# Longer buffers in the ring of split weights, and attention outputs placed elsewhere in memory

## The chip, the cores and the metric

The kernel runs on one core of a Trainium2 chip. The metric is the time of one execution in device microseconds (us), as the median of several runs. Besides the timed runs there is one profiled execution, whose trace the rows below come from; its own time stands beside its span in the table.

## What is computed

Two transformer-like blocks follow one another on 256 tokens of width 1024 (plus 16 learned tokens ahead of them), all in fp32. Cut to what matters here:

```python
# first block
proj = rms_norm(h) @ w_in                       # two convolution branches follow
h = h + concat(norm(y_sc), norm(y_cf)) @ w_out
hn = rms_norm(h)
idx, gates = route(hn @ w_q, sub_keys)          # top 16 of 16384 experts for each of 8 heads
act = gelu(einsum(u[idx], hn))
h = h + einsum(act * gates, v[idx])             # u and v: 16384 x 1024
# second block
proj = rmsnorm(h) @ w_in_2                      # 6144 columns: two attentions
y_sb, y_df = o_sb @ w_br_sb, o_df @ w_br_df     # outputs of the two attentions
merged = gates_a * y_sb + gates_b * y_df
h = h + merged @ w_out_2
h = h + (silu(hn @ w_ffn_gate) * (hn @ w_ffn_up)) @ w_ffn_down
```

The kernel multiplies with all 16384 experts and lets the gates be zero elsewhere, so that `u` and `v` are two matrices of 128 pieces each.

## The kernel before

Every weight matrix is cut into units of 128 x 1024 fp32 numbers; there are 454 of them, in an order written out in the list `units`. A unit goes through three rings of buffers. SyncE's queue loads it into one of 5 buffers `raw`. ScalarE copies it, rounded, into one of 3 buffers `hi` (line 152), and VectorE writes what the rounding left into one of 3 buffers `lo` (line 154). A product is then three matmuls: hi with hi, hi with lo, lo with hi, added in PSUM. Activations are kept in such pairs too: `hT` (input of `q`, `u`, `fg` and `fu`), `xT` and `xT2` (inputs of the two first projections, with 272 columns to a chunk), `osb` and `odf` (the outputs of the two attentions, inputs of `ysb` and `ydf`).

Two helpers issue nearly all matmuls. In `mm_w` the unit is the stationary operand, 128 columns at a time, and the activations stream past it:

```python
for k in range(KC):                                   # 8 chunks of 128
    ks = slice(k * P, (k + 1) * P)
    nc.tensor.matmul(ps, hi[:, ks], ahi[:, k, cols], ...)   # L183
    nc.tensor.matmul(ps, hi[:, ks], alo[:, k, cols], ...)   # L184
    nc.tensor.matmul(ps, lo[:, ks], ahi[:, k, cols], ...)   # L185
```

In `mm_a` (L197 to L199) the unit streams, 512 columns at a time, past 128 columns of activations: `v` past `w_hi` and `w_lo`, `fd` past `f_hi` and `f_lo`, `o` past `mghi` and `mglo`, `wo` past `yhi` and `ylo`. While one matmul streams, TensorE loads the stationary operand of the next, so that two reads of the core's working memory run side by side.

TensorE and SyncE follow the order in which the code is written; the other engines' order comes from a scheduler. Between the matmuls of `u` some small ones stand: the scores `sc`, and from about 370 us on the gates `gp` (L712), in the middle of every unit.

Where a tile lies is decided by pools, which place tiles one behind another. In bytes from the start of a partition, before the change: `hThi` 11168 and `hTlo` 8192 bytes behind it; the three `hi` buffers 48608, 52704, 56800; the three `lo` buffers 60896, 64992, 69088; `w_hi` 204256 (two buffers of 2048 bytes); `osbhi` 121696; `odfhi` 138080; `xT2hi` 103200; the first `f_hi` 110368; `mghi` 170848; `yhi` 182048. The buffers of a ring are 4096 bytes apart.

Of the kernel before, what the change touches and what calls it, by code (L numbers as in the profile page):

```python
# [9 lines left out]
F32 = mybir.dt.float32  # L10
F32R = mybir.dt.float32r
# [8 lines left out]
P = 128  # L20
D = 1024
# [14 lines left out]
XN = 2  # L36
WARM = 9
SOON = 60

_VECS = [  # L40
    ("norm_mix_g", 8), ("norm_mix_g_2", 8), ("b_gate_2", 16),
# [11 lines left out]
def two_blocks(ctx, tc, x, feats, vecs, w_in, w_out, w_q, keys, u, v, final_g, meta2, w_in2, lams, w_gate,  # L53
# [3 lines left out]
    const = ctx.enter_context(tc.tile_pool(name="const", bufs=1))  # L57
    wraw = ctx.enter_context(tc.tile_pool(name="wraw", bufs=5))
    whi = ctx.enter_context(tc.tile_pool(name="whi", bufs=3))
    wlo = ctx.enter_context(tc.tile_pool(name="wlo", bufs=3))  # L60
# [4 lines left out]
    def phase(name):  # L65
        st = ExitStack()
        pool = st.enter_context(tc.tile_pool(name=name, bufs=1, reuse_waits="tile"))
        return st, pool

    def mm_tile(name):  # L70
        return pmm.tile([P, 512], F32, tag="mm", name=name)
# [42 lines left out]
    loaded, ready, used = [], [], [0]  # L114
    held, latest = [], {}

    def queued(after):
        st = ExitStack()
        for i in after:
            st.enter_context(tc.issue_after(i.ins))  # L120
        return st

    def soon(i):
        return tc.high_priority(offset=SOON) if 30 <= i < 172 else ExitStack()

# [12 lines left out]

    def split_part(half):
        if half == 0:  # L140
            ready.append((whi.tile([P, D], F32R, tag="hi", name="hi0"), wlo.tile([P, D], F32R, tag="lo", name="lo0")))
        hs = slice(half * 512, (half + 1) * 512)
        hi, lo = (o[:, hs] for o in ready[0])
        nc.scalar.activation(hi, loaded[0][:, hs], AF.Copy)
        nc.vector.tensor_tensor(lo, loaded[0][:, hs], hi.bitcast(F32), op=ALU.subtract)

    def split_to(n):
        while len(ready) < min(n, len(units)):
            i = len(ready)
            with queued(held), soon(i):  # L150
                hi = whi.tile([P, D], F32R, tag="hi", name=f"hi{i}")
                latest["hi"] = nc.scalar.activation(hi, loaded[i], AF.Copy)  # L152
                lo = wlo.tile([P, D], F32R, tag="lo", name=f"lo{i}")
                latest["lo"] = nc.vector.tensor_tensor(lo, loaded[i], hi.bitcast(F32), op=ALU.subtract)  # L154
            ready.append((hi, lo))

    def unit(ahead=2):
        n = used[0]
        used[0] += 1
        load_to(n + 5)  # L160
        split_to(n + 1 + ahead)
        held.clear()
        return ready[n]
# [131 lines left out]


    s_x, px = phase("px")
    s_c, pc = phase("pc")
    load_part(0)
    load_part(1)  # L300
# [22 lines left out]
    for c in range(KC):  # L323
        g = col("norm_mix_g", c)
        nc.scalar.activation(xT[0][:, c, :], xf[:, c, :], AF.Copy, scale=g)
        nc.vector.scalar_tensor_tensor(xT[1][:, c, :], xf[:, c, :], g, xT[0][:, c, :].bitcast(F32),
                                       op0=ALU.mult, op1=ALU.subtract)
        if c in (1, 3):
            split_part(c // 2)
    split_to(2)  # L330
    for c in range(0, KC, 2):
        nc.scalar.activation(sq[:, c:c + 2, :], xf[:, c:c + 2, :], AF.Square)
# [183 lines left out]


    s_a, pa = phase("pa")
    NA = 96
    ew = [pa.tile([P, T // 4, NA, 4], F32, tag="ewa", name="ewa"), None]  # L520
# [5 lines left out]

    lm = pr.tile([P, 4, 64], F32, tag="lm", name="lm")
    nc.sync.dma_start(lm, lams.broadcast_to((P, 4, 64)))
    lam = const.tile([P, 1], F32, tag="lam", name="lam")
    sg8 = const.tile([P, 1], F32, tag="sg8", name="sg8")  # L530

    vals_a = pr.tile([P, 2, NH, TOPK], F32, tag="vals", name="vals")
    pos_a = pr.tile([P, 2, NH, TOPK], U32, tag="pos", name="pos")
# [312 lines left out]
    s_q, pq = phase("pq")  # L846
# [43 lines left out]
    NQ = sum(QN)  # L890
    QS = slice(NM, L)

    osb = (pq.tile([P, NH, T], F32R, tag="osbhi", name="osbhi"), pq.tile([P, NH, T], F32R, tag="osblo", name="osblo"))
    odf = (pq.tile([P, NH, T], F32R, tag="odfhi", name="odfhi"), pq.tile([P, NH, T], F32R, tag="odflo", name="odflo"))
    gate = pq.tile([P, 16, T], F32, tag="gate", name="gate")
    s_sb, psb = phase("psb")
# [362 lines left out]
```

## Time and profile before

| | |
|---|---|
| median of 3 runs | 1456.65 us (1452.66 to 1460.02) |
| the profiled execution | 1458.39 us |
| its span, first to last instruction | 1456.4 us |
| mean granted TensorE clock | 0.997 of full speed |
| TensorE busy (matmul) | 1437.3 us, 99% of the span |
| VectorE, ScalarE busy | 72%, 51% |
| matmuls in the trace | 10114 |

The span is 2.0 us short of the execution's own time, and that execution lies 1.7 us above the median. A matmul's duration in the trace runs from its start to its modelled end, and matmuls overlap: one of 256 columns is listed with some 0.28 us while the next starts about 0.115 us after it. What a matmul costs is therefore the distance between two starts, not its listed duration.

### The profile page before, as it was taken

To read this page: it belongs to the slowest core of one execution; us is meant where nothing else is said; L and a number is where in the kernel's file an instruction comes from. 1 tells how busy PE (TensorE), PEld (TensorE's weight loads), DVE (VectorE), ACT (ScalarE), POOL (GpSimd) and SP (SyncE) were. 2 spreads that over 40 slices of the span, in tenths; PEclk is the share of its full clock that TensorE was granted. 3 is DMA by queue.
4 is the path that set the end of the run, shared out by engine and by line. 5 is a ranking of instruction groups with operands and counts; after the bars stand their busy time and mean duration, and the time that the engine had idled before them with its cause. 6 is when DMAs were issued, how large, how long until landed. Compare 5 with 4: busy or idle time off the path is not lost.

```text
span 1456.4 us, 25587 instructions
## 1 busy us (share of the span) xinstructions
PE 1437.3 (99%) x10114; PEld 1340.5 (92%) x10114; DVE 1050.6 (72%) x1887; ACT 742.9 (51%) x1236; POOL 14.5 (1%) x35
## 2 busy tenths in 40 slices
PE   8999999999999999999999999999999999999998
PEld 8988999999999999888888888899999999899997
DVE  8997789894988999655555565675577776765666
ACT  7555444554444444444444544564455674554444
POOL 0010000000000000000000000000000000000000
PEclk9999999999999999999999999999999999999999
DMA  7525655666444444566666676654344456556562
GB/s 242 198 73 185 183 181 176 193 196 194 147 138 137 145 136 141 174 189 200 190 189 200 190 249 196 189 174 129 119 130 131 131 174 188 165 185 195 184 197 103
DMA packets 69816, 248.96 MB, mean 171 GB/s; under 512 B 7744, under 2 KB 9152, under 8 KB 69696
## 3 DMA queue, kind: packets, MB, share of 16 engines
q1 hardware_dynamic: 68256, 242.61, 53.5%
q0 software_dynamic: 1152, 4.19, 0.8%
q8 instruction: 79, 1.29, 0.4%
q10 hardware_dynamic: 288, 0.52, 0.1%
q14 instruction: 41, 0.34, 0.1%
HBM read 245.20 MB, written 2.10 MB: 170 GB/s over the span
## 4 chain that ended last, share of the span: by engine, by line
PE 92%; DVE 6%; issue 1%; ACT 0%; DMA 0%; SPq 0%; DVEq 0%; ACTq 0%
PE v L198 8%; PE v L197 8%; PE v L199 8%; PE u L183 7%; PE u L185 7%; PE u L184 7%; PE gp L712 4%; DVE lo L154 2%; PE fg L184 1%; PE fg L185 1%; PE fg L183 1%; PE fu L184 1%; PE fu L183 1%; PE fu L185 1%; PE fd L199 1%; PE fd L198 1%
## 5 line engine op out<-in xcount | busy, mean ns | idle before, releaser
L154 DVE TENSOR_TENSOR lo<-raw,hi 128x1024 fp32r<-128x1024 f32 x453 | 551.7, 1223 | 250.1 <-ACT hi L152 248.1
L152 ACT ACTIVATE hi<-raw 128x1024 fp32r<-128x1024 f32 x453 | 476.4, 1057 | 429.8 <-PE u L184 124.8
L183 PE MATMUL u<-hThi,hi 128*128 128x256 f32 x1024 | 297.3, 290 | 0.0
L185 PE MATMUL u<-hThi,lo 128*128 128x256 f32 x1024 | 286.9, 280 | 0.1
L184 PE MATMUL u<-hTlo,hi 128*128 128x256 f32 x1024 | 286.5, 280 | 0.0
L199 PE MATMUL v<-hi,w_lo 128*128 128x512 f32 x512 | 199.2, 389 | 0.0
L198 PE MATMUL v<-lo,w_hi 128*128 128x512 f32 x512 | 199.2, 389 | 0.0
L197 PE MATMUL v<-hi,w_hi 128*128 128x512 f32 x512 | 199.2, 389 | 0.0
L185 PEld LDWEIGHTS u<-hThi,lo 128*128 128x128 f32 x1024 | 193.7, 189 | 0.6 <-DVE lo L154 0.3
L184 PEld LDWEIGHTS u<-hTlo,hi 128*128 128x128 f32 x1024 | 194.2, 190 | 0.0
L183 PEld LDWEIGHTS u<-hThi,hi 128*128 128x128 f32 x1024 | 192.8, 188 | 0.0
L197 PEld LDWEIGHTS v<-hi,w_hi 128*128 128x128 f32 x512 | 96.1, 188 | 20.0
L199 PEld LDWEIGHTS v<-hi,w_lo 128*128 128x128 f32 x512 | 96.1, 188 | 20.0
L198 PEld LDWEIGHTS v<-lo,w_hi 128*128 128x128 f32 x512 | 96.1, 188 | 19.7
L712 PE MATMUL gp<-ga,gb 128*128 128x128 f32 x512 | 74.8, 274 | 0.0
L712 PEld LDWEIGHTS gp<-ga,gb 128*128 128x128 f32 x512 | 66.2, 190 | 0.0
L810 ACT ACTIVATE w_hi<-ewa 128x512 fp32r<-128x512 f32 x48 | 30.4, 633 | 65.9 <-PE v L198 65.9
L812 DVE TENSOR_TENSOR w_lo<-ewa,w_hi 128x512 fp32r<-128x512 f32 x48 | 33.2, 692 | 38.6 <-ACT w_hi L810 38.6
L184 PE MATMUL fg<-hTlo,hi 128*128 128x256 f32 x176 | 48.9, 278 | 0.4 <-DVE hTlo L245 0.4
L183 PE MATMUL fg<-hThi,hi 128*128 128x256 f32 x176 | 48.9, 278 | 0.3 <-ACT hThi L244 0.3
L185 PE MATMUL fg<-hThi,lo 128*128 128x256 f32 x176 | 48.9, 278 | 0.0
L183 PE MATMUL fu<-hThi,hi 128*128 128x256 f32 x176 | 48.7, 277 | 0.0
(409 smaller groups left out, 2949.8 us busy)
## 6 DMA issues: line engine op xcount, KB each, us to landing
raw<-in_u_dram SPq DMA_DIRECT2D x128, 512.0 KB, 3.6
raw<-in_v_dram SPq DMA_DIRECT2D x128, 512.0 KB, 3.6
raw<-in_w_in_dram SPq DMA_DIRECT2D x67, 512.0 KB, 3.6
raw<-in_w_fg_dram SPq DMA_DIRECT2D x22, 512.0 KB, 4.2
raw<-in_w_fu_dram SPq DMA_DIRECT2D x22, 512.0 KB, 3.6
raw<-in_w_fd_dram SPq DMA_DIRECT2D x22, 512.0 KB, 4.5
raw<-in_w_out_dram SPq DMA_DIRECT2D x16, 512.0 KB, 3.6
raw<-in_w_q_dram SPq DMA_DIRECT2D x16, 512.0 KB, 4.1
```

What stands on the lines that cost most here:

```text
L152: latest["hi"] = nc.scalar.activation(hi, loaded[i], AF.Copy)
L154: latest["lo"] = nc.vector.tensor_tensor(lo, loaded[i], hi.bitcast(F32), op=ALU.subtract)
L183: nc.tensor.matmul(ps, hi[:, ks], ahi[:, k, cols], start=(k == 0), stop=False)
L184: nc.tensor.matmul(ps, hi[:, ks], alo[:, k, cols], start=False, stop=False)
L185: nc.tensor.matmul(ps, lo[:, ks], ahi[:, k, cols], start=False, stop=(k == KC - 1))
L197: nc.tensor.matmul(ps, ahi[:, ts], hi[:, bs], start=first and n == 0, stop=False)
L198: nc.tensor.matmul(ps, ahi[:, ts], lo[:, bs], start=False, stop=False)
L199: nc.tensor.matmul(ps, alo[:, ts], hi[:, bs], start=False, stop=end)
L712: nc.tensor.matmul(p3[:, :, i], b[:, i, :], a[:, i, :], start=True, stop=True)
L810: nc.scalar.activation(hi, a, AF.Copy)
L812: nc.vector.tensor_tensor(lo, a, hi.bitcast(F32), op=ALU.subtract)
```

## The change

Each tile of the rings `hi` and `lo` gets 16 more fp32 numbers (64 bytes) that nothing uses, so that the buffers of a ring are 4160 bytes apart. The two small constants `lam` and `sg8` become two columns of one tile, which takes 32 bytes less. Two unused tiles, of 576 and 896 bytes, are placed ahead of `osb` and `odf`.

```diff
+SKEW = 16
+OSB, ODF = 576, 896
...
+    def fill(pool, n, name):
+        pool.tile([P, n // 4], F32, tag=name, name=name)
+
+    def ring(pool, tag, name):
+        return pool.tile([P, D + SKEW], F32R, tag=tag, name=name)[:, :D]
...
-                hi = whi.tile([P, D], F32R, tag="hi", name=f"hi{i}")
+                hi = ring(whi, "hi", f"hi{i}")
                 latest["hi"] = nc.scalar.activation(hi, loaded[i], AF.Copy)
-                lo = wlo.tile([P, D], F32R, tag="lo", name=f"lo{i}")
+                lo = ring(wlo, "lo", f"lo{i}")
...
-    lam = const.tile([P, 1], F32, tag="lam", name="lam")
-    sg8 = const.tile([P, 1], F32, tag="sg8", name="sg8")
+    lam_sg = const.tile([P, 2], F32, tag="lam_sg", name="lam_sg")
+    lam, sg8 = lam_sg[:, 0:1], lam_sg[:, 1:2]
...
+    fill(pq, OSB, "osb_at")
     osb = (pq.tile([P, NH, T], F32R, tag="osbhi", name="osbhi"), pq.tile([P, NH, T], F32R, tag="osblo", name="osblo"))
+    fill(pq, ODF, "odf_at")
     odf = (pq.tile([P, NH, T], F32R, tag="odfhi", name="odfhi"), pq.tile([P, NH, T], F32R, tag="odflo", name="odflo"))
```

After it, in bytes: `hThi` 11168 as before; `hi` 48576, 52736, 56896; `lo` 61056, 65216, 69376; `w_hi` 204608; `osbhi` 122624; `odfhi` 139904; `xT2hi` 103552; the first `f_hi` 110720; `mghi` 172672. Everything allocated behind `sg8` thus lies at a multiple of 64 bytes where it lay 32 bytes past one, except `yhi` and `ylo` of the second branch, where it is the other way round; `hT` stays 32 bytes past one.

No instruction is added, and the order of TensorE, VectorE, GpSimd and SyncE is the same. One pair moves: the two copies of the 16 learned tokens into `xT2`. On ScalarE before, where `hi267` to `hi299` are the last units of `v`, 33 splits of such units stand behind them:

```order
L152 ACTIVATE hi265_9260<-raw265_9218 128x1024
L810 ACTIVATE w_hi94_9276<-ewa_1330 128x512
L152 ACTIVATE hi266_9282<-raw266_9240 128x1024
L849 ACTIVATE xT2hi_10008<-m2hi_1022 128x8x16
L849 ACTIVATE xT2lo_10009<-m2lo_1023 128x8x16
L152 ACTIVATE hi267_9300<-raw267_9258 128x1024
```

On ScalarE after, one split of a unit of `v` (`hi299`) stands behind them:

```order
L160 ACTIVATE hi297_9899<-raw297_9857 128x1024
L818 ACTIVATE w_hi126_9915<-ewb_4410 128x512
L160 ACTIVATE hi298_9921<-raw298_9879 128x1024
L857 ACTIVATE xT2hi_10007<-m2hi_1022 128x8x16
L857 ACTIVATE xT2lo_10008<-m2lo_1023 128x8x16
L160 ACTIVATE hi299_9939<-raw299_9897 128x1024
L295 ACT_TABLE_LOAD
```

They moved 32 units later on the same engine, and nothing else changed places.

## Rows read from the trace of the kernel before

**Rows 1.** The page: busy time of each engine, and TensorE's clock in 40 slices.

```profile
span 1456.4 us, 25587 instructions
...
PE 1437.3 (99%) x10114; PEld 1340.5 (92%) x10114; DVE 1050.6 (72%) x1887; ACT 742.9 (51%) x1236; POOL 14.5 (1%) x35
...
PEclk9999999999999999999999999999999999999999
```

**Rows 2.** The page: shares of the chain that ended last.

```profile
PE 92%; DVE 6%; issue 1%; ACT 0%; DMA 0%; SPq 0%; DVEq 0%; ACTq 0%
```

**Rows 3.** TensorE, timeline of a unit of `q`: start, duration (us).

```profile
190.43 0.28 PE L185 MATMUL q<-hThi,lo 128*128 128x256 f32 x1
...
193.26 0.28 PE L185 MATMUL q<-hThi,lo 128*128 128x256 f32 x1
```

**Rows 4.** The same, for a unit of `u` some 95 us later.

```profile
285.42 0.28 PE L185 MATMUL u<-hThi,lo 128*128 128x256 f32 x1
...
288.14 0.28 PE L185 MATMUL u<-hThi,lo 128*128 128x256 f32 x1
```

**Rows 5.** TensorE's groups, 124 to 247 us: count, busy us, mean ns of one, idle.

```profile
L184 PE MATMUL u<-hTlo,hi 128*128 128x256 f32 x230 | 64.6, 281 | 0.0
...
L184 PE MATMUL q<-hTlo,hi 128*128 128x256 f32 x96 | 27.9, 291 | 0.0
```

**Rows 6.** The same, 250 to 302 us.

```profile
L184 PE MATMUL u<-hTlo,hi 128*128 128x256 f32 x113 | 31.2, 276 | 0.0
```

**Rows 7.** The same, 370 to 585 us.

```profile
L184 PE MATMUL u<-hTlo,hi 128*128 128x256 f32 x453 | 127.3, 281 | 0.0
L185 PE MATMUL u<-hThi,lo 128*128 128x256 f32 x453 | 127.1, 281 | 0.0
L712 PE MATMUL gp<-ga,gb 128*128 128x128 f32 x496 | 72.4, 274 | 0.0
```

**Rows 8.** TensorE's groups over the whole span, by shape: matmuls of 256 and 272 columns.

```profile
L185 PE MATMUL u<-hThi,lo 128*128 128x256 f32 x1024 | 286.9, 280 | 0.1
L184 PE MATMUL u<-hTlo,hi 128*128 128x256 f32 x1024 | 286.5, 280 | 0.0
...
L184 PE MATMUL fg<-hTlo,hi 128*128 128x256 f32 x176 | 48.9, 278 | 0.4 <-DVE hTlo L245 0.4
...
L185 PE MATMUL fu<-hThi,lo 128*128 128x256 f32 x176 | 48.6, 276 | 0.0
...
L184 PE MATMUL g<-xT2lo,hi 128*128 128x256 f32 x128 | 35.9, 281 | 0.0
...
L399 PE MATMUL conv<-up,diag 128*128 128x256 f32 x86 | 18.9, 378 | 0.0
...
L184 PE MATMUL ydf<-odflo,hi 128*128 128x256 f32 x64 | 18.0, 282 | 0.0
L185 PE MATMUL ysb<-osbhi,lo 128*128 128x256 f32 x64 | 18.0, 281 | 0.0
...
L184 PE MATMUL ps_sk<-xT2lo,hi 128*128 128x272 f32 x64 | 18.5, 288 | 0.0
```

**Rows 9.** The same view: matmuls of 512 columns, where the unit streams.

```profile
L199 PE MATMUL v<-hi,w_lo 128*128 128x512 f32 x512 | 199.2, 389 | 0.0
L198 PE MATMUL v<-lo,w_hi 128*128 128x512 f32 x512 | 199.2, 389 | 0.0
L197 PE MATMUL v<-hi,w_hi 128*128 128x512 f32 x512 | 199.2, 389 | 0.0
...
L198 PE MATMUL fd<-lo,f_hi 128*128 128x512 f32 x88 | 34.7, 394 | 0.0
...
L199 PE MATMUL wo<-hi,ylo 128*128 128x512 f32 x32 | 12.7, 398 | 0.8 <-DVE ylo L469 0.8
...
L199 PE MATMUL o<-hi,mglo 128*128 128x512 f32 x32 | 12.6, 394 | 0.0
```

**Rows 10.** TensorE, timeline in the middle of `v`.

```profile
601.31 0.39 PE L199 MATMUL v<-hi,w_lo 128*128 128x512 f32 x1
...
606.07 0.39 PE L199 MATMUL v<-hi,w_lo 128*128 128x512 f32 x1
```

**Rows 11.** TensorE, timeline of six fp32 passes of the convolution, merged.

```profile
34.72 1.46 PE L399 MATMUL conv<-up,diag 128*128 128x256 f32 x6
```

**Rows 12.** ScalarE, timeline around the two copies; in brackets the idle time ahead.

```profile
848.48 0.29 ACT L849 ACTIVATE xT2hi<-m2hi 128x128 fp32r<-128x128 f32 x1
848.67 0.29 ACT L849 ACTIVATE xT2lo<-m2lo 128x128 fp32r<-128x128 f32 x1
849.93 1.06 ACT L152 ACTIVATE hi<-raw 128x1024 fp32r<-128x1024 f32 x1 [0.96 <-PE v L199]
```

More of the change, by code (lines that the diff above doesn't have):

```diff
@@ L140, in split_part @@
         if half == 0:
-            ready.append((whi.tile([P, D], F32R, tag="hi", name="hi0"), wlo.tile([P, D], F32R, tag="lo", name="lo0")))
+            ready.append((ring(whi, "hi", "hi0"), ring(wlo, "lo", "lo0")))
         hs = slice(half * 512, (half + 1) * 512)
```

## The prediction

> **What bounds the kernel now.** I read the page first: TensorE is busy 99% of the span, at full clock in every slice [rows 1], and the chain that ended last is 92% TensorE [rows 2]. VectorE at 72% and ScalarE at 51% have room. So the time is the number of matmuls, which stays, times the distance from one start to the next, and the change can act only on that distance.
>
> So I went to the timeline. In a unit of `q`, 24 matmuls take from 190.43 to 193.26 us [rows 3]: 2.83 us / 24 = 118 ns each. In a unit of `u`, with the same tile `hT`, the same rings and the same 256 columns, 24 take from 285.42 to 288.14 us [rows 4]: 113.3 ns. The groups say the same: a listed duration of 281 ns goes with 118 and one of 276 ns with 113.3, so a difference between listed means is a difference between distances wherever nothing is waited for. By that measure the stretch from 124 to 247 us runs at 281 throughout, that from 250 to 302 us at 276 [rows 5, 6], and that from 370 to 585 us, with gates in the middle of each unit, at 281 again [rows 7]. Other engines do not explain a pace that stays put for 120 us. What I read in it: two reads of working memory run side by side in TensorE, the streaming operand and the next stationary one; they can settle into a rhythm without collisions or into one with them; and the rhythm survives from unit to unit.
>
> **What the rhythm could have to do with addresses.** Chunks of a unit are 512 bytes apart and chunks of `hT` 1024, so unit address minus activation address, modulo 512, is the same for all chunks. Before, all six buffers share it: `hT` 64, `osb` and `odf` 128, `v` 0, `fd` 192, `o` 128, `wo` 192 (worked out from the addresses above; `xT2` has chunks 1088 bytes apart and sweeps through all multiples of 64). The rows beside it: distance 0 gives 389 ns for 512 columns in all three lines of `v`, while 128 and 192 give 394 to 398 [rows 9]; `v` takes 4.76 us for 21 matmuls, 226.7 ns each [rows 10]. Distance 128 gives 281 to 282 at 256 columns (`ysb`, `ydf`), the sweep 281 (`g`), distance 64 both 276 and 281, and in `fg` and `fu` nearly always the good one, 276 to 278 [rows 8]. After, the six differ: `hT` sees 32, 160, 96 from `hi` and 224, 352, 288 from `lo`; `v` sees 128, 256, 192 and 320, 448, 384; `osb` 192, 320, 256 and 384, 0, 448; `odf` 320, 448, 384 and 0, 128, 64 (in the order of the three buffers' use).
>
> **The change part by part.** I use 276.2 ns (48.6 us / 176) as the good duration.
>
> `u`: L184 and L185 have 286.5 and 286.9 us for 1024 each, 280.0 ns, so 3.8 ns over; for three lines, 3072 x 3.8 = 11.7 us at most. Of this, the stretch with gates holds 452 x 3 x 4.8 = 6.5 us, and the rest 5.2. `q`: 96 of its 128 in each line lie in the slow stretch, 288 x 4.8 = 1.4 us (its listed 291 contains waits). If the collisions live on because every unit lies at the same distance, distances that change from unit to unit should break them up. Bounds: 0 and 13.1 us. I take all of 5.2 and 1.4, since `fu` shows that the good rhythm can hold for long, and half of 6.5, since the gates restart the stream in every unit and it may fall either way. 9.9 us.
>
> `ysb` and `ydf`: 384 matmuls, 5.3 ns over: 2.0 us at most, 0 at least; I take 2.0, as these two tiles are both moved and skewed.
>
> `v`: 0. It runs at its best row now and can gain nothing from a better rhythm. Bound on the other side: 1536 x 5 ns (394 - 389) = 7.7 us, with `wo`'s 398 13.8 us. `fg` and `fu`: 0, bound 1056 x 4 = 4.2 us of loss. `fd`, `o`, `wo`: 456 matmuls, +-5 ns, 2.3 us either way; 0. `g` and the 272-column projections sweep before and after: 0.
>
> The two copies moved on ScalarE take 0.29 us each and stand ahead of an idle time of 0.96 us [rows 12]; later they delay the split of unit 299 by at most 0.59 us, and splits run two units of 5.4 us (24 x 226.7 ns) ahead. Nothing, unless that lead were gone: then 0.6 us. The merged constants and the unused tiles add no instruction. Writing rings at other addresses could change VectorE's and ScalarE's own durations, which the trace can't show; with both engines off the chain [rows 2] I take 0.
>
> Sum: 9.9 + 2.0 = 11.9 us. 1458.4 - 11.9 = 1446.5 for an execution like the profiled one; that one lies 1.7 above the median, so 1445.
>
> One rule speaks against all of it. The Trainium skill, "TensorE: Matmul & The Clock Gate", section "Step-by-step: what each phase is for", says that TensorE has two independent read ports and that loading the next weights takes no read bandwidth from the running matmul. By that the sum would be 0. That the same matmul on the same tiles goes at 113.3 and 118 ns [rows 3, 4] shows that something disturbs it, though not that it is the other read.
>
> **The rivals.** *Slower: `v` loses its rhythm.* `v` is the one long stream at distance 0, and every 512-column stream at another distance is slower by 5 to 9 ns [rows 9]. After the change none of the six buffers is at 0 from `w_hi`. Then `v` pays 7.7 us; if `fg` and `fu` go to 281 as well, 4.2; if `u` and `q`, instead of gaining, run wholly at 281 to 282, 3456 x 1.3 = 4.5. All three are one mechanism, that only a constant, fortunate distance keeps a rhythm free of collisions: 7.7 + 4.2 + 4.5 = 16.4, so 1473. With my gain in `u` kept, it decides from 11.9 us / 1536 = 7.7 ns on a matmul of `v`. For it: `v`, `fd`, `o` and `wo`. Against: the slow stretch of `u` at a constant distance.
>
> *No change.* Either distances don't matter, and the two paces come from how a stream started (the unchanged addresses of rows 3 and 4 speak for it), or `u` gains what `v` loses (11.9 - 7.7 = 4.2): 1452 to 1457.
>
> *Much faster: a lower floor.* Nearly all tiles but `hT` move from 32 bytes past a multiple of 64 to a multiple of 64. Were 113.3 and 226.7 ns themselves the price of that offset, `v` would fall. How far, bounded by the row that streams slowest per column: a pass of the convolution, six of which take 1.46 us with a tail of 378 ns [rows 8, 11], starts every 216 ns. `v` at 216 saves 1536 x 10.7 = 16.4 us, with the 11.9 above 1428. No row before has an aligned stream in this format, so nothing speaks for or against it directly. The same page, section "Back-to-back issue gap", has N/2.4 + 2.5 ns, or 216 ns for 512 columns and 109 for 256; by its figures `v` would save an estimated 16.9 us. Distances of exactly 113.3 and 226.7 disagree with it before the change.
>
> **How the numbers follow.** Forecast (1439 to 1449) 0.34; much faster 0.11; no change or an even trade (1449.5 to 1464) 0.26; slower 0.29. 0.5% is 7.3 us, about what can be told from no change. Faster is the forecast and the lower floor, 0.45; slower is the rival, 0.29; same 0.26. The range reaches from the lower floor's 1428 to the rival's 1474 and leaves out under 2 in 10 in the tails (a lower floor in the other streams too, or `v` at `wo`'s 398). The forecast's own range is 1439 to 1449.
>
> **What would show it.** Right: `u`'s L184 and L185 at 276 to 278 instead of 280, also from 370 to 585 us; `ysb` and `ydf` at 276 to 278; `v` at 389; clock and order as before. Wrong: `v` at 393 or more (the rival), `u` still at 280 or more, or a listed duration below 276 or 389 (the lower floor). The step I trust least is that varied distances break up a collision rhythm in `u` and leave `v` alone: `v`'s own row is the evidence against it.

## The result, and the profile after

| | before | after |
|---|---|---|
| median of 4 runs (before: the 3 above and one more) | 1457.77 us (1452.66 to 1460.02) | 1470.67 us (1469.51 to 1473.88) |
| profiled execution, its span | 1458.39, 1456.4 us | 1473.88, 1471.8 us |
| mean granted TensorE clock | 0.997 | 0.995 |

The ratio is 1.0095, with a 95% interval from 1.0069 to 1.012: slower, by 0.95%, where the forecast was faster. The median lies inside the stated range, but 21 us above the forecast's own (1439 to 1449). The page after, the engines' line and the chain:

```profile
span 1471.8 us, 25586 instructions
...
PE 1454.7 (99%) x10114; PEld 1353.7 (92%) x10114; DVE 1051.2 (71%) x1887; ACT 742.6 (50%) x1236; POOL 15.6 (1%) x35
...
PE 92%; DVE 5%; ACT 1%; DMA 1%; issue 1%; SPq 0%; POOL 0%; DVEq 0%; ACTq 0%
```

TensorE is the bound as before, with as many matmuls, and busy 17 us longer; VectorE and ScalarE have the same work in the same time. The groups of TensorE by shape (busy us, mean ns of one), which answer to [rows 8, 9]; lines have moved by 8:

```profile
L193 PE MATMUL u<-hThi,lo 128*128 128x256 f32 x1024 | 288.1, 281 | 0.0
L192 PE MATMUL u<-hTlo,hi 128*128 128x256 f32 x1024 | 287.9, 281 | 0.0
L206 PE MATMUL v<-lo,w_hi 128*128 128x512 f32 x512 | 201.5, 393 | 0.4 <-DVE lo L162 0.4
L205 PE MATMUL v<-hi,w_hi 128*128 128x512 f32 x512 | 200.8, 392 | 0.0
L207 PE MATMUL v<-hi,w_lo 128*128 128x512 f32 x512 | 200.7, 392 | 0.0
...
L192 PE MATMUL fg<-hTlo,hi 128*128 128x256 f32 x176 | 49.5, 281 | 0.4 <-DVE hTlo L253 0.4
...
L193 PE MATMUL fu<-hThi,lo 128*128 128x256 f32 x176 | 49.3, 280 | 0.0
...
L192 PE MATMUL ydf<-odflo,hi 128*128 128x256 f32 x64 | 17.9, 280 | 0.0
```

`v` has gone from 389 to 392 or 393, `fu` from 276 to 280, `fg` from 278 to 281, and `u`, forecast at 276 to 278, to 281. The pace itself is in the timeline of TensorE after, a stretch of `u` and the first two units of `v`:

```profile
283.82 0.28 PE L191 MATMUL u<-hThi,hi 128*128 128x256 f32 x1
...
292.35 0.28 PE L191 MATMUL u<-hThi,hi 128*128 128x256 f32 x1
...
600.73 0.39 PE L205 MATMUL v<-hi,w_hi 128*128 128x512 f32 x1
...
606.25 0.40 PE L205 MATMUL v<-hi,w_hi 128*128 128x512 f32 x1
```

The first two rows are three units apart, 72 matmuls: 8.53 us / 72 = 118.5 ns, where [rows 4] had 113.3 in this part of the span. The last two are 24 matmuls apart: 230.0 ns, where [rows 10] had 226.7.

Where the time went, by the first start of a stage in the two traces (us):

| stage | before | after | difference |
|---|---|---|---|
| up to `q` | 124.21 | 123.72 | -0.5 |
| `q` and `u`, up to `v` | 472.6 | 477.0 | +4.4 |
| `v`, up to `ps_sq` | 351.2 | 357.5 | +6.3 |
| projections and `g`, up to `ysb` | 247.5 | 249.2 | +1.7 |
| `ysb`, `ydf`, `o`, up to `fg` | 70.9 | 70.5 | -0.4 |
| `fg`, `fu`, `fd`, to the end | 190.0 | 193.9 | +3.8 |

The sum is 15.4 us (before rounding), the difference of the two spans. The +1.7 of the projections is not the change's. The stretches after (PEclk is the granted clock as a share of 2.4 GHz):

```profile
core 0: us, PE busy (x) PEld busy (x) DVE busy (x) ACT busy (x) POOL busy (x), PEclk, DMA share, GB/s
950.00:958.00 8.00, 7.40 (x40) 5.87 (x38) 6.79 (x12) 5.00 (x12) 0.31 (x1) 1.00 0.43 131
958.00:959.30 1.30, 0.61 (x4) 0.24 (x2) 1.30 (x3) 1.29 (x3) 0.24 (x1) 1.00 0.19 38
959.30:963.50 4.20, 4.20 (x23) 4.20 (x24) 4.05 (x5) 1.40 (x2) 0.00 (x0) 0.59 0.65 204
963.50:970.00 6.50, 6.50 (x55) 6.50 (x54) 5.09 (x15) 5.34 (x13) 0.53 (x1) 1.00 0.66 229
```

Behind a start of `ps_sq` with little work ahead (0.61 us in 1.3), the clock stood at 0.59 for 4.2 us, most of it at its lower level of 1.2 GHz: 15 matmuls 0.213 us apart instead of 0.118, with the two at its edges 1.6 us. The same place in the kernel before, with as little work ahead (0.49 us in 1.1), and in the kernels with one half of the change kept the full clock. So 13.8 us remain for the change in this profile, and 12.9 between the medians.

### The profile page after: what moved, and what is told of

The parts are those of the page before. It is cut to its first block, busy times and chain, and to the rows that moved or that the text cites. A ratio compares the mean times of both kernels' runs of the same rounds, so it can differ in the third digit from the quotient of the medians.

```text
span 1471.8 us, 25586 instructions
## 1 busy us (share of the span) xinstructions
PE 1454.7 (99%) x10114; PEld 1353.7 (92%) x10114; DVE 1051.2 (71%) x1887; ACT 742.6 (50%) x1236; POOL 15.6 (1%) x35
## 4 chain that ended last, share of the span: by engine, by line
PE 92%; DVE 5%; ACT 1%; DMA 1%; issue 1%; SPq 0%; POOL 0%; DVEq 0%; ACTq 0%
PE v L206 8%; PE v L205 8%; PE v L207 8%; PE u L191 7%; PE u L192 7%; PE u L193 7%; PE gp L720 4%; DVE lo L162 1%; PE fg L192 1%; PE fu L191 1%; PE fu L192 1%; PE fu L193 1%; PE fg L191 1%; PE fg L193 1%; PE fd L207 1%; PE fd L206 1%
## 5 line engine op out<-in xcount | busy, mean ns | idle before, releaser
L192 PE MATMUL fu<-hTlo,hi 128*128 128x256 f32 x176 | 49.5, 281 | 0.0
```

Source lines behind the costliest of these rows:

```text
L192: nc.tensor.matmul(ps, hi[:, ks], alo[:, k, cols], start=False, stop=False)
```

## The experiments

The theories: *changing* (distances that differ from buffer to buffer keep TensorE out of its free rhythm), *distance* (each distance of unit and activation has a pace of its own), *alignment* (multiples of 64 bytes). Distances are unit minus activation, modulo 512. A pace is called free when it is the fastest that was seen, 113.3 ns for 256 columns and 226.7 for 512. Each ratio is to the kernel before as timed on the same chip beside that run. Its median there was 1451.37 us for the first four experiments, 1454.5 for those from the skew of 256 bytes to the moved stages, 1454.79 for the first two versions with kicks and 1455.6 for the last two.

**The skew undone.** The changed kernel with one number altered.

```diff
-SKEW = 16
+SKEW = 0
```

> The changed kernel with ring buffers 4096 bytes apart again; the merged constants (everything behind them at a multiple of 64 bytes) and the two fills stay. Distance of unit minus activation, modulo 512, is the same for all buffers again: 32 for hT, 0 for v, 64 for osb, 192 for odf. Theory 'changing' (the loss comes from distances that differ from buffer to buffer, which keep TensorE from settling): v back at 389 ns, u at 276 to 281, fg and fu at 276 to 279, time 1452 to 1461. Theory 'alignment' (the loss comes from tiles at multiples of 64 bytes): v at 392 to 393, u, fg and fu at 281, time 1468 to 1474. Theory 'distance' (a value of its own for each distance, 0 the only free one): v at 389, but u, fg and fu at 281 since 32 is not 0; time about 1463.

1467.31 us, ratio 1.0108 (1.0077 to 1.0140).

```profile
L192 PE MATMUL u<-hTlo,hi 128*128 128x256 f32 x1024 | 287.7, 281 | 0.0
L207 PE MATMUL v<-hi,w_lo 128*128 128x512 f32 x512 | 199.2, 389 | 0.0
...
L192 PE MATMUL fu<-hTlo,hi 128*128 128x256 f32 x176 | 49.4, 281 | 0.0
```

`v`, back at the constant distance 0 and now at multiples of 64 bytes, is back at 389: alignment neither slows it nor gives it a lower floor. The ring and `w_hi` both lie 32 bytes lower than in the kernel before, so `v` kept its pace with its distance and not with an address. `u` and `fu`, at the constant distance 32 instead of 64, are at 281 all the same. A constant distance is not enough.

**The skew alone.** The kernel before with `ring` and `SKEW = 16`; no merged constants, no fills.

> The kernel before with ring buffers 4160 bytes apart and nothing else: tiles stay 32 bytes past a multiple of 64, osb and odf have no fill. 'Changing': v at 392 to 393, u, fg, fu at 281, time 1468 to 1474. 'Alignment': v at 389, u at 280, fu at 276, time 1453 to 1460. 'Distance': v at 391 to 394, u, fg, fu 280 to 281, time 1466 to 1474 (does not part it from 'changing').

1468.6 us, ratio 1.0116 (1.0083 to 1.0148); `v` at 392 to 393, `fu` at 281, `u` at 280:

```profile
L188 PE MATMUL u<-hTlo,hi 128*128 128x256 f32 x1024 | 287.0, 280 | 0.0
L202 PE MATMUL v<-lo,w_hi 128*128 128x512 f32 x512 | 201.4, 393 | 0.0
...
L188 PE MATMUL fu<-hTlo,hi 128*128 128x256 f32 x176 | 49.5, 281 | 0.0
```

Each half alone costs about as much as both. The merged constants take `u`, `fg` and `fu` off the distance 64 altogether. The skew leaves one of three `hi` and one of three `lo` buffers at it and moves the others off, and it takes `v` off 0 as well.

**`u`, `ysb`, `ydf` and `o` at distance 0 too.** The kernel before, with two fills; `v` stays at 0, `fd` and `wo` keep their distances.

```diff
+    fill(const, 448, "ring_at")
...
+    fill(pq, 128, "osb_at")
```

> The kernel before with a fill of 448 bytes behind hT and one of 128 bytes ahead of osb, so that the units lie at distance 0 modulo 512 from hT, osb, odf and mg, as they do from w_hi; ring buffers 4096 bytes apart. 'Distance' (0 is free of collisions): u and q without waits at 276, fu and fg 276, ysb and ydf 276, o at 389; u saves 11, q 1.4, ysb and ydf 2, fg 1: time 1441 to 1445. 'Changing' alone (any constant distance may fall either way): u between 276 and 281 in stretches as before, ysb and ydf perhaps still 281, time 1450 to 1460. 'Alignment': no change, 1453 to 1460.

1471.95 us, ratio 1.0145 (1.0113 to 1.0177): a miss for all three theories as I had put them.

```profile
L187 PE MATMUL u<-hTlo,hi 128*128 128x256 f32 x1024 | 289.5, 283 | 0.0
...
L202 PE MATMUL v<-hi,w_lo 128*128 128x512 f32 x512 | 199.2, 389 | 0.0
...
L188 PE MATMUL fu<-hThi,lo 128*128 128x256 f32 x176 | 49.8, 283 | 0.0
...
L202 PE MATMUL o<-hi,mglo 128*128 128x512 f32 x32 | 12.4, 389 | 0.0
```

Where the unit streams, 0 is the free distance: `o`, at 393 to 395 before, is at 389 to 391. Where activations stream past the unit, 0 is worse than any before: `u`, `fu`, `ysb` and `ydf` all at 283. So a distance has a pace of its own, but 0 is not the free one for both kinds of stream.

**`v` at another constant distance.** A fill of 128 bytes ahead of `w_hi`.

> The kernel before with a fill of 128 bytes ahead of w_hi and w_lo, so that every unit of v lies at the constant distance of 384 modulo 512 (128 the other way) from them, the distance that osb and o have before. 'Changing' alone: constant, so v stays at 389 and the time at 1453 to 1460. 'Distance': v at 392 to 395, 5 to 9 us more, time 1461 to 1468. 'Alignment': no change.

1462.81 us, ratio 1.0077 (1.0049 to 1.0106).

```profile
L187 PE MATMUL u<-hTlo,hi 128*128 128x256 f32 x1024 | 283.4, 277 | 0.0
...
L200 PE MATMUL v<-hi,w_hi 128*128 128x512 f32 x512 | 202.0, 395 | 0.0
```

All six buffers still share one distance, and `v` takes 395. So the loss does not need distances that change. The profiled execution was at 1457.77, 5 us under the median; in it `u`, whose addresses are untouched, ran at 277, where [rows 8] had 280. At its distance of 64 it has stood at either pace, by the profile that one looks at.

**A skew of 256 bytes.** The skew alone with `SKEW = 64`; for the room, `raw` has 4 buffers.

> The kernel before with ring buffers 4352 bytes apart (64 more numbers each instead of 16), for which the ring raw gives up one of its 5 buffers. Distances now change from buffer to buffer, but only by 256 bytes: v at 0 or 256, u at 64 or 320 (unit minus activation, modulo 512). Theory 'distance modulo 256' (the value decides, not that it changes): v at 389, fg and fu 276 to 279, u 276 to 281 as before, time 1450 to 1460, unless the missing raw buffer shows as waits of the splits for transfers. Theory 'changing': v at 392 to 393, u at 281, time 1466 to 1472. If the period is 512, v is slow where the distance is 256.

1453.99 us, ratio 1.0000 (0.9979 to 1.0021).

```profile
L188 PE MATMUL u<-hTlo,hi 128*128 128x256 f32 x1024 | 285.3, 279 | 0.0
L202 PE MATMUL v<-lo,w_hi 128*128 128x512 f32 x512 | 199.3, 389 | 1.0 <-DVE lo L158 1.0
...
L188 PE MATMUL fu<-hTlo,hi 128*128 128x256 f32 x176 | 48.6, 276 | 0.0
```

The distances change from buffer to buffer by 256 and nothing is lost: that is the end of "changing". Between 0 and 256, and between 64 and 320, there is no difference, so from here on distances are given modulo 256.

**`u` at 96 and at 160.** Fills of 32 and of 96 bytes behind `hT`.

> The kernel before with a fill of 32 bytes behind hT: units of q, u, fg, fu at the constant distance 96 from hT instead of 64. 'Distance': its own constant value; so far 64 gave 276 or 281, 32 gave 281 and 0 gave 283, so 96 may be free in all restarts (u 276, some 1446 to 1449) or not (281, 1462 to 1467); v 389 either way. 'Changing' (a constant distance can settle): u partly at 276.

> The same with a fill of 96 bytes: distance 160. 'Distance': its own value, between 276 (about 1447) and 283 (about 1470); ysb and ydf stand at 128 before, at 281 to 282, so 281 is the likelier. v 389 either way.

One run each, 1466.86 and 1472.56 us, with `u` at 281 and at 283, `fu` at 280 and 283 (L187):

```profile
L187 PE MATMUL u<-hTlo,hi 128*128 128x256 f32 x1024 | 287.4, 281 | 0.0
```

```profile
L187 PE MATMUL u<-hTlo,hi 128*128 128x256 f32 x1024 | 289.3, 283 | 0.0
```

**The other stages at their free distances.** Fills of 64 bytes ahead of `osb`, 64 ahead of `mg`, 192 ahead of `f_hi`; the ring as before.

> The kernel before with three fills that move no ring: osb and odf to the distance 64 that u, fg and fu have (64 bytes ahead of osb), mg and f_hi, f_lo to the distance 0 that v has (64 bytes ahead of mg, 192 ahead of f_hi). 'Distance': o and fd fall from 394 to 396 to 389 to 391 (351 matmuls by 5 ns, 1.8 us); ysb and ydf either 276 or 281 (0 to 2.0 us); together 2 to 4 us less than the kernel before, ratio 0.997 to 0.999, u as before by chance at 276 or 281. 'Changing': no difference in o and fd.

1456.77 us, ratio 1.0022 (1.0005 to 1.0038), where I had expected 0.997 to 0.999: a miss. `o` and `fd` are at 389 as expected, but TensorE's groups from 1295 to 1430 us, where `fd` stands between units of `fg` and `fu`, read:

```profile
L187 PE MATMUL fg<-hTlo,hi 128*128 128x256 f32 x129 | 36.2, 281 | 0.0
...
L188 PE MATMUL fu<-hThi,lo 128*128 128x256 f32 x128 | 36.0, 281 | 0.0
L200 PE MATMUL fd<-hi,f_hi 128*128 128x512 f32 x66 | 25.7, 389 | 0.0
```

Over the span of this profile, `fd` and `o` gain 264 x 5 and 96 x 5 ns, 1.8 us, and `fg` and `fu` lose 528 x 3 and 528 x 4, 3.7 us, at an unchanged distance. `ysb` and `ydf`, now at 64, stayed at 281. So a distance of 64 allows the free pace and does not assure it. That `fd`'s own pace is what slowed `fg` and `fu` is not shown: the profile with 18 kicks below has both at 281 with `fd` at 394 to 396.

**The two reads by themselves.** A kernel of its own, which leaves out all of the two blocks. Its operands are all ones, and for each kind of stream its core is:

```python
for d in range(0, 256, 16):
    for n in (128, 112, 96, 80, 64, 120):
        kick(n)      # one matmul of n columns
        one(d)       # 24 matmuls of 256 columns (or 12 of 512)
        one(d)
```

> Not the reference's work: the kernel computes nothing of it and writes zeros. TensorE alone runs the two kinds of stream, with no other engine at work, at 16 distances (unit minus activation, 0 to 240 in steps of 16 bytes): activations of 256 columns past a unit, and units of 512 columns past activations; 6 series of 48 or 24 matmuls for each, each begun behind one matmul of another length (128, 112, 96, 80, 64, 120 columns), so that it starts at another phase. If the two reads inside TensorE are the cause: 256 columns take 113.3 ns at 64 in some or all series, 117 to 118 at 32 and 96, 120 at 0; 512 columns take 226.7 at 0 and 230 to 232 at 128, 64 and 192. Distances between the steps that the kernels had may be free whatever the start. If splits, copies or transfers of other engines are the cause: 113.3 and 226.7 at all distances.

Some of its groups (the number in the name is the distance; each holds the six starts):

```profile
L81 PE MATMUL act_past_unit_at_000x<-act,wgt 128*128 128x256 f32 x288 | 35.3, 284 | 0.0
...
L81 PE MATMUL act_past_unit_at_096x<-act,wgt 128*128 128x256 f32 x288 | 34.8, 282 | 0.0
...
L90 PE MATMUL unit_past_act_at_192x<-wgt,act 128*128 128x512 f32 x144 | 34.4, 398 | 0.0
...
L90 PE MATMUL unit_past_act_at_064x<-wgt,act 128*128 128x512 f32 x144 | 33.8, 394 | 0.0
L81 PE MATMUL act_past_unit_at_064x<-act,wgt 128*128 128x256 f32 x288 | 33.7, 278 | 0.0
L90 PE MATMUL unit_past_act_at_000x<-wgt,act 128*128 128x512 f32 x144 | 33.5, 392 | 0.0
```

After the operands are filled no other engine works, and the paces differ as in the kernels above. From one start to the next, in the second half of the series, where the start has worn off (ns, worked out from the starts in the trace; the steps between, 16, 48, ..., lie at 116.7 or more and at 230.0 or more):

| distance modulo 256 | 0 | 32 | 64 | 96 | 128 | 160 | 192 | 224 |
|---|---|---|---|---|---|---|---|---|
| 256 columns past a unit | 120.0 | 118.3 | 113.3, once 117.8 | 117.4 to 118.8 | 118.7 | 120.0 | 117.8 | 116.7 or 117.8 |
| unit, 512 columns | 226.7 | 233.3 | 228.9 | 233.3 | 233.0 | 234.3 | 233.3 | 233.3 |

Of the 16 distances each kind has exactly one free one, 64 and 0, and the kernel before has `u`, `q`, `fg`, `fu` at the one and `v` at the other. With the table the change can be added up. `v` after sees 128, 0, 192 from `hi` (two of three matmuls) and 64, 192, 128 from `lo`: (2 x 231.0 + 231.7) / 3 = 231.2 ns, 4.5 more, 7.0 us. Its stage grew by 6.3, and its starts lie 230.4 apart over the stage, so the table, taken at constant distances, is a little high here. `u` sees 32, 160, 96 and 224, 96, 32: 118.5 ns by the table, 118.5 in the timeline above. Streams of the kernel before agree too: `ysb` and `ydf`, at 128, start 118.7 and 118.5 ns apart, and `wo`, at 192 in the first branch and 160 in the second, 233.8.

**The rhythm and the start.** The same kernel with `one(64)` alone, behind 14 kinds of kick in a mixed order.

> Not the reference's work: zeros are written, and TensorE alone runs streams of 256 columns at distance 64, 168 series of 48 matmuls, each behind one matmul of another length (rounded format: 32 to 128 columns; full fp32, two passes: 32, 64, 128 columns), in a mixed order. At 64 both rhythms exist (113.3 and 117.8 ns). If the rhythm is settled by the phase at which a series starts and then kept: every series ends at exactly 113.3 or 117.8, and the length of the matmul ahead, with the rhythm before it, decides which: the same pair leads to the same rhythm each time. If it is chance: the same pair leads to both. A length that leads to 113.3 from either rhythm would be a means to get u, fg and fu into the free rhythm.

Every series ended at 113.3 (113 of them) or at 117.8 (55), and for each length and each rhythm before it the outcome was the same every time. Timeline of TensorE, series merged:

```profile
143.25 0.22 PE L76 MATMUL kick_round_112x<-act 128*128 128x112 f32 x1
143.30 5.88 PE L83 MATMUL act_past_unit_at_064x<-act,wgt 128*128 128x256 f32 x48
149.01 0.20 PE L76 MATMUL kick_round_088x<-act 128*128 128x88 f32 x1
149.05 5.70 PE L83 MATMUL act_past_unit_at_064x<-act,wgt 128*128 128x256 f32 x48
...
171.50 0.22 PE L76 MATMUL kick_round_112x<-act 128*128 128x112 f32 x1
171.55 5.88 PE L83 MATMUL act_past_unit_at_064x<-act,wgt 128*128 128x256 f32 x48
```

112 columns lead out of the free rhythm (5.88 us) and 88 back into it (5.70). From the slow rhythm 112 columns led into the free one, so the rhythm before counts as well as the length. Lengths from 64 to 104, and 120, led into the free rhythm from either side, for some 0.13 us each (from their start to that of the 25th matmul behind them, less 24 x 113.3).

**Kicks in the kernel.** The kernel before, with a matmul of 88 columns ahead of some units (its result is overwritten).

```diff
+KICK = range(28, 172, 16)
...
         ahi, alo = a
+        if used[0] - 1 in KICK:
+            nc.tensor.matmul(ps[:, :88], hi[:, :P], hi[:, :88], start=True, stop=True)
         for k in range(KC):
```

> The kernel before, with one extra matmul of 88 columns ahead of every 16th unit of q and u (9 in all; its result is overwritten). Addresses as before. If the length of a matmul decides the rhythm that follows at distance 64, as in the run with the kicks, each puts q and u into 113.3 ns for 0.13 us: u's L184, L185 at 276 to 278 (280 before), the stage at 5 to 10 us less than the profile of before, and fewer slow runs: 1448 to 1452, ratio 0.996 to 0.999. If the rhythm is lost again soon after each, or chosen by something else in the kernel: as before, 1451 to 1457, u at 279 to 281.

> The same ahead of every 8th unit (18 in all): 1.2 us more for the kicks. If the rhythm lasts 16 units after a kick: 1449 to 1453. If it is lost after some 8 units: faster than with 9 kicks, 1448 to 1451.

1453.39 us, ratio 0.9992 (0.9979 to 1.0006), and 1453.62, ratio 0.9993 (0.9978 to 1.0009): not to be told from before. In both profiles `u` was at 277 over the whole span, as hoped. But so it was in the profile with `v` at 128, with no kick at all, so these profiles do not show that the kicks did it. With 18 kicks `fg` and `fu` stood at 281:

```profile
L187 PE MATMUL u<-hTlo,hi 128*128 128x256 f32 x1024 | 283.5, 277 | 0.0
...
L188 PE MATMUL fg<-hThi,lo 128*128 128x256 f32 x176 | 49.5, 281 | 0.0
L188 PE MATMUL fu<-hThi,lo 128*128 128x256 f32 x176 | 49.5, 281 | 0.0
L200 PE MATMUL fd<-hi,f_hi 128*128 128x512 f32 x88 | 34.7, 394 | 0.0
```

**Kicks in `fg` too, and fewer in `u`.** `KICK = [*range(28, 172, 16), 388, 398, 422]`, then `[30, 72, 94, 112, 388, 398, 422]`.

> The kernel with 9 kicks, and three more ahead of units of fg (the first, and two among those between which fd stands): 0.4 us more. If executions near 1457 come from fg and fu in the slow rhythm: all near 1451 to 1453, median 1451.5 to 1452.5, ratio 0.997 to 0.999, fg and fu at 276 to 279. If they come from elsewhere (clock, transfers): both groups stay, median 1453 to 1454.

> 7 kicks only: 4 in q and u, where the rhythm was lost in other profiles (the start, behind the waits near 260 and 310 us, the first gates), and the three of fg. If u keeps its rhythm between them: 0.7 us less than the run with 12 kicks, 1450.5 to 1452. If not: u partly at 281, 1452 to 1456.

1453.29 us, ratio 0.9984 (0.9967 to 1.0001), and 1452.97 us, ratio 0.9976 (0.9957 to 0.9995), the one version of four that the measurement puts ahead of the kernel before, by 0.24%, with an interval that ends just short of no change. In both profiles `fu` was at 276 and `fg` at 278, and yet the executions still spread from 1449.56 to 1457.91 with 7 kicks. In the profile with 7 kicks `u` (L187) was still slow from 124 to 247 us, and free from 430 to 585:

```profile
L187 PE MATMUL u<-hTlo,hi 128*128 128x256 f32 x238 | 66.8, 281 | 0.0
...
L187 PE MATMUL u<-hTlo,hi 128*128 128x256 f32 x334 | 92.7, 277 | 0.0
```

So a kick that always led into the free rhythm with TensorE alone does not do so in the kernel. What else decides there was not found.

## Why the prediction was wrong

**What bounds the kernel** held: the same matmuls, the same clock but for 4 us at `ps_sq` and less than 1 us at `q`, and the rest of the difference in the distance of starts. "Full clock in every slice" was read too finely, though. In both profiles the granted clock stood at 0.50 from 124 to 126 us, in the first unit of `q`. Some 20 matmuls there start 213 ns apart before, and 12 after, so the stage of `q` and `u` gained some 0.8 us after that is not the change's. The listed 291 of `q` [rows 5], which the prediction puts down to waits, has this low clock in it; its idle time is 0.0.

**`u` and `q`: forecast -9.9, measured +4.4.** This is the step that failed: "If the collisions live on because every unit lies at the same distance, distances that change from unit to unit should break them up." They live on at most distances, constant or not. I had the two paces at one distance [rows 3, 4] and took the constancy for the cause of the slow one. The scan shows the reverse: 64 is the one distance at which the fast pace exists at all. Which of the two paces a stream has at 64 comes, with TensorE alone, from what ran ahead of it, as the series with the kicks show; in the kernel it was not found. Moving the units off 64 removes the choice and leaves the slow pace. That this cost only 4.4 us is luck of the one profile before, where most of `u` was slow already. In the profile with `v` at 128, with the addresses of `q` and `u` untouched, their stage took 463.5 us, 9.1 less than in the profile before and 13.5 less than after the change (about 2.0 and 1.2 of that are the low clock at `q`, which that profile lacks). Most of the gain that I forecast was there to be had, at the very distance that the change took away.

**`v`: forecast 0, bound +7.7, measured +6.3.** The bound was right and its cause too: 0 is the only free distance where a unit streams, and after the change two of the three `hi` buffers and all three `lo` buffers are off it. (The prediction says that none of the six is at 0; the one at 256 is, as the skew of 256 bytes shows.) The row that showed it, `v` at its best at 0 and every other distance behind it [rows 9], stood in the text as evidence for the rival. I let `u` outweigh it.

**`fg` and `fu`: forecast 0, bound 4.2; the stage grew by 3.8**, from 276 to 278 up to 280 or 281, as the bound had it: off 64 there is no free pace.

**`ysb` and `ydf`: forecast -2.0; the stage with `o` fell by 0.4.** They went from 281 or 282 to between 279 and 281: from one slow distance to several, some a little better.

**`fd`, `o`, `wo`, `g`: forecast 0.** `o` and `fd` could gain, though little from varied distances, by which only one line of `fd` moved clearly, from 394 to 390: at 0 they fell to 389. `wo`, which the prediction puts at 192, is there in its first branch alone; nothing in the sum hangs on it.

**The moved copies** stood at 945.7 us and are part of no loss that shows: the groups of `v` have 0.4 us of waits on a split in all.

**The rivals.** The slower one, priced at 16.4 us and 1473, is what happened: 15.4 between the spans (1.6 of them the clock) and 1470.67. Term by term it had 4.5, 7.7 and 4.2 for what came to 4.4, 6.3 and 3.8; the first is luck, as said above. Its mechanism was put a little wrong, as "only a constant, fortunate distance": fortunate it must be, constant it need not be, as the skew of 256 bytes shows. "Much faster" fell with `v` at 389 on multiples of 64 bytes. "An even trade" needed a gain in `u` that no distance but 64 can give. The slower rival's chance, 0.29, was too low: two of the longest free streams, `v` and `fu`, spoke for it, and only a reading of `u` against.

**The rule.** By the Trainium skill, "TensorE: Matmul & The Clock Gate", section "Step-by-step: what each phase is for", the load of the next weights takes nothing from the running matmul. With TensorE alone at work the same matmul of 256 columns took 113.3 to some 120 ns, by the distance of its two operands' addresses and by what ran ahead. Here the measurement speaks against the rule. That it is the load's read which disturbs the stream is the likely reading, but no trace shows the two reads themselves.

Still open: what in the memory has a period of 256 bytes, and whether the operand that counts is the next stationary one or the present one; in these streams both lie at the same distance modulo 512.

## What to carry to other kernels

When TensorE bounds a kernel and two stretches of the same matmul run at different paces, look at the addresses of the two operands before the order of the work: scan their distance in a kernel that does nothing else, for each shape of stream. Place the tiles by the table only with a timing of the whole kernel beside it: here, moving `fd`, `o`, `ysb` and `ydf` to their free distances made the kernel 0.22% slower, not faster. A layout that looks regular may stand at the best distance already, and a few bytes ahead of it, in a constant that has nothing to do with it, take it away. Two edits that each spoil the same thing cost no more together than alone, so undo a change in halves before adding up its parts.

## What the runs showed of the hardware

- The distance of streaming and stationary operand, modulo 256 bytes, goes with the pace: 113.3 to some 120 ns for 256 columns in the rounded format, 226.7 to some 235 for 512, with TensorE alone at work. Of 16 distances the free one is 64 for the one and 0 for the other.
- At 64 there are two rhythms, 113.3 and 117.8 ns. In the kernel either one held for hundreds of matmuls. With TensorE alone, the length of a single matmul ahead and the rhythm before it decided, the same way in all 168 series, which one followed.
- Taking a stage to its free distance need not gain time: with `fd` at 389 instead of 394 to 396, `fg` and `fu` between its pieces stood at 281 in the profile instead of 276 to 278, and the kernel was no faster. Whether the one caused the other is open.
